# Seven block products in place of eight for m W_o in a hybrid decoder layer, with the norm chains rewritten and moved

## The chip, the core and the metric

One core of a Trainium2 chip runs the whole program: TensorE (PE) multiplies, VectorE (DVE), ScalarE (ACT) and GpSimd (POOL) work on SBUF and PSUM, SyncE (SP) issues DMAs. The metric is the device time of one execution in microseconds (us), median of several. Numbers are fp32 on the outside; lower is better.

## What is computed

One decoder layer for 512 tokens of width 1024. Cut to what matters:

```python
h = rms_norm(x, g_pre_mix)
q, k, v, cb, cc, cu, ga, gc = split(h @ w_in)
y_attn = stick_breaking_attention(q, k, v) @ w_attn_out      # 8 heads x 64
y_conv = (cb * causal_depthwise_conv(cc * cu)) @ w_conv_out  # 512 channels
m = sigmoid(ga + b) * y_attn + sigmoid(gc + b) * y_conv
x = x + rms_norm(m @ w_o, g_post_mix)                        # w_o: 1024 x 1024
x = x + rms_norm(relu(rms_norm(x, g_pre_mlp) @ w_up) ** 2 @ w_down, g_post_mlp)   # 4096 wide
x = x + sigmoid(rms_norm(x, g_ple) @ w_ple_gate) * (p @ w_ple_proj)
```

## The kernel before

Each fp32 operand is split into a high part, rounded to PE's format by ACT, and the rest, made by DVE (`split`, lines 63 to 66); `mm3` (lines 90 to 93) multiplies high x high, high x low and low x high into one PSUM bank, so every product is three matmuls. A weight block comes by a DMA on SP's queue into one of four `raw` buffers and is split into two of 15 `w` buffers of 128 x 1024 (`weights`, `wcols`, `wrow`; `w4` is such a buffer as 2 x 512). Sixteen `big` buffers of 128 x 2048 hold what lives longer; PSUM has eight banks of 128 x 512, taken by `bank()`.

The stages on PE, in order: the head (norm of x, v), attention in four steps j of two heads each, mix in eight steps j of 128 columns of m (two gate products, y_conv's and y_attn's), W_o, p's product with w_pp, W_up, W_down, the last gate. PE's and SP's instructions run in the order in which the program writes them (`manual_schedule`, line 41). DVE, ACT and POOL are ordered by a scheduler when the program is built, from its own costs and the order of the text; `tc.issue_after(ins)` puts the instructions of a block behind `ins` on its engine. On every engine that order is then fixed, and an instruction that waits holds those behind it.

W_down is already multiplied as 2 x 2 blocks by seven products instead of eight, and W_up (from column block 2) as well: sums and differences of blocks are multiplied and added up onto each other's banks. W_down's sums of weight blocks are made early: `make_sums` (line 296) loads two blocks of w_down (512 KB each), makes four differences of 128 x 512 on DVE or POOL, and its results are saved to DRAM by the next `save_sums` (line 289). It is called 16 times: twice before attention, once in each step of attention, once in each of mix (on POOL from j = 2 on), and twice in W_o.

Around the change. In mix (line 468) each m block [128 channels x 512 tokens] is split into `m_h` and `m_l`. At j = 3 x is loaded again (`xr`, four DMAs of 512 KB), at j = 6 p and w_pp, at j = 7 p is turned by eight PE transposes (line 497). `rows` (line 501) is W_o: for the first four blocks of k all four token tiles and both column halves, into eight banks; then, token tile by token tile, the last four blocks of k, and behind each tile its `chain1`: `residual` (line 539) squares both banks on ACT, adds the sums up, takes the power -1/2 on POOL, scales and multiplies by the gain on DVE, adds x, squares again, scales again. `turn2` (line 563) turns a token tile's 1024 normed values by eight transposes into two banks and splits them; turn2(0) and turn2(1) stand in W_o, turn2(2) in p's product, turn2(3) in W_up's first matmuls. W_up's column blocks 0 and 16 go in two halves of 256 tokens, so that their upper half can start early; block 1 and 17 go whole; `relu2` (line 600) takes relu on ACT and the square on DVE. `residual1` (line 531) is the same chain behind W_down.

## Time and profile before

| | us |
|---|---|
| median of 3 runs | 737.27 (736.19 to 740.18) |
| the profiled execution | 735.77 |
| its span, first to last instruction | 734.0 |
| PE busy | 725.5 |
| DVE busy | 518.3 |
| ACT busy | 379.3 |
| POOL busy | 93.8 |

The profile is of one execution. Its span leaves out what lies before the first and behind the last instruction. "Busy" is the time in which at least one instruction of an engine was under way; matmuls overlap, so a matmul's busy time is longer than the distance to the next. In a row of a group, after the bar, stand the total busy time, the mean of one in ns, and the idle time of the engine just before them with what ended it. `L91` is line 91 of the kernel; `ps<-whi,mh` says that `ps` is written from `whi` and `mh`.

### The profile page before, as it was taken

The page shows a single profiled execution, that of the slowest core. Times are in us where ns is not written, and L with a number is a line of the kernel's source. Part 1 is how long each engine was busy: PE and PEld are TensorE (multiplying, and loading weights), DVE is VectorE, ACT ScalarE, POOL GpSimd, SP SyncE. Part 2 cuts the span into 40 slices and gives each one's busy share as a digit, 9 for nine tenths or more (in the row PEclk, how much of TensorE's full clock was granted, in tenths as well). Part 3 has the DMA queues.
Part 4 walks back from the last instruction along what each step waited for, and adds up shares of the span by engine and source line. Part 5 has one row for each costly group of instructions (what it writes and reads, how often), then busy time and mean ns, then how long its engine had stood idle before and what let it go on. Part 6 is the DMA issues. An engine that isn't in the chain of part 4 may idle for free.

```text
span 734.0 us, 10311 instructions
## 1 busy us (share of the span) xinstructions
PE 725.5 (99%) x3976; PEld 628.9 (86%) x3976; DVE 518.3 (71%) x644; ACT 379.3 (52%) x595; POOL 93.8 (13%) x120
## 2 busy tenths in 40 slices
PE   8999999999999999999999999999999999999997
PEld 7888788888888888888899999999988888888886
DVE  6777886968555534734789988976799778269762
ACT  6245446352434323433856777756867476256431
POOL 1106061433225220001100000000000000001100
PEclk9999999999999999999999999999999999999999
DMA  8595627154999966752424445523455767577311
GB/s 315 171 303 166 184 96 225 35 200 144 290 346 328 282 217 243 250 165 72 153 92 115 116 117 142 138 66 111 147 172 185 238 223 231 179 242 268 127 57 58
DMA packets 112105, 132.29 MB, mean 180 GB/s; under 512 B 4116, under 2 KB 82744, under 8 KB 111032
## 3 DMA queue, kind: packets, MB, share of 16 engines
q1 hardware_dynamic: 111464, 127.43, 54.8%
q10 hardware_dynamic: 592, 4.20, 1.4%
q8 instruction: 31, 0.51, 0.3%
q14 instruction: 18, 0.15, 0.1%
HBM read 108.55 MB, written 23.07 MB: 179 GB/s over the span
## 4 chain that ended last, share of the span: by engine, by line
PE 96%; DVE 1%; DMA 1%; ACT 1%; issue 0%; POOL 0%; DVEq 0%; SPq 0%; ACTq 0%; POOLq 0%
PE ps L91 30%; PE ps L92 30%; PE ps L93 30%; DMA raw<-in_w_conv_out_dram 1%; PE ps L340 1%; PE ps L388 1%; PE ps L374 1%; PE ps L182 1%; DVE wlo L65 1%; PE ps L568 1%; PE ps L141 0%; PE ps L201 0%; PE ps L223 0%; ACT whi L64 0%; PE ps L497 0%
## 5 line engine op out<-in xcount | busy, mean ns | idle before, releaser
L65 DVE TENSOR_TENSOR wlo<-raw,whi 128x512 fp32r<-128x512 f32 (+1 forms) x84 | 79.2, 964 | 54.0 <-ACT whi L64 42.0
L91 PE MATMUL ps<-h1h,whi 128*128 128x512 f32 x288 | 113.3, 393 | 0.9 <-DVE st L65 0.9
L93 PE MATMUL ps<-h1h,wlo 128*128 128x512 f32 x288 | 112.2, 390 | 0.0
L92 PE MATMUL ps<-h1l,whi 128*128 128x512 f32 x288 | 112.2, 389 | 0.0
L64 ACT CAST whi<-raw 128x512 fp32r<-128x512 f32 (+1 forms) x84 | 65.4, 808 | 60.8 <-DMA raw<-in_w_in_dram 29.0
L91 PE MATMUL ps<-w,sb 128*128 128x512 f32 x216 | 84.1, 389 | 0.0
L93 PE MATMUL ps<-w,sb 128*128 128x512 f32 x216 | 84.0, 389 | 0.0
L92 PE MATMUL ps<-w,sb 128*128 128x512 f32 x216 | 84.0, 389 | 0.0
L65 DVE TENSOR_TENSOR w<-raw,w 128x1024 fp32r<-128x1024 f32 x56 | 67.7, 1221 | 21.2 <-PE ps L92 10.2
L64 ACT CAST w<-raw 128x1024 fp32r<-128x1024 f32 x56 | 58.5, 1052 | 36.1 <-PE ps L93 13.6
L133 POOL TENSOR_TENSOR rs<-ms,mhalf 128x1 f32<-128x1 f32 x20 | 14.6, 729 | 440.0 <-DVE ms L129 364.7
L91 PEld LDWEIGHTS ps<-h1h,whi 128*128 128x128 f32 x288 | 54.1, 188 | 12.5 <-DVE st L65 1.1
L93 PEld LDWEIGHTS ps<-h1h,wlo 128*128 128x128 f32 x288 | 54.1, 188 | 11.4
L92 PEld LDWEIGHTS ps<-h1l,whi 128*128 128x128 f32 x288 | 54.1, 188 | 10.9
L92 PE MATMUL ps<-h2l,us 128*128 128x256 f32 x224 | 63.4, 283 | 0.0
L91 PE MATMUL ps<-h2h,us 128*128 128x256 f32 x224 | 63.4, 283 | 0.0
L93 PE MATMUL ps<-h2h,us 128*128 128x256 f32 x224 | 63.4, 283 | 0.0
L65 DVE TENSOR_TENSOR us<-raw,us 128x1024 fp32r<-128x1024 f32 x42 | 50.7, 1220 | 7.9 <-ACT us L64 7.8
L64 ACT CAST us<-raw 128x1024 fp32r<-128x1024 f32 x42 | 43.4, 1050 | 17.1 <-PE ps L93 6.3
L93 PEld LDWEIGHTS ps<-w,sb 128*128 128x128 f32 x216 | 40.5, 188 | 8.5
L92 PEld LDWEIGHTS ps<-w,sb 128*128 128x128 f32 x216 | 40.5, 188 | 8.4
L91 PE MATMUL ps<-tb,us 128*128 128x256 f32 x168 | 47.7, 284 | 0.0
(206 smaller groups left out, 1650.8 us busy)
## 6 DMA issues: line engine op xcount, KB each, us to landing
raw<-in_w_in_dram SPq DMA_DIRECT2D x36, 512.0 KB, 7.0
w<-in_w_down_dram SPq DMA_DIRECT2D x32, 512.0 KB, 4.5
wsum<-w SPq DMA_DIRECT2D x32, 512.0 KB, 4.0
raw<-in_w_up_dram SPq DMA_DIRECT2D x32, 512.0 KB, 4.2
raw<-wsum SPq DMA_DIRECT2D x32, 512.0 KB, 5.3
raw<-in_w_down_dram SPq DMA_DIRECT2D x24, 512.0 KB, 4.1
raw<-in_w_o_dram SPq DMA_DIRECT2D x8, 512.0 KB, 5.9
raw<-in_w_ple_gate_dram SPq DMA_DIRECT2D x8, 512.0 KB, 7.1
```

The costliest lines, as they stand in the source:

```text
L64: a = nc.scalar.copy(hi, src)
L65: b = nc.vector.tensor_tensor(lo, src, hi.bitcast(F32), op=ALU.subtract)
L91: nc.tensor.matmul(ps, lh, rh, start=start, stop=False, skip_group_check=onto)
L92: nc.tensor.matmul(ps, lh, rl, start=False, stop=False, skip_group_check=onto)
L93: nc.tensor.matmul(ps, ll, rh, start=False, stop=stop, skip_group_check=onto)
L133: nc.gpsimd.tensor_tensor(r, m, mhalf, op=ALU.pow)
L182: nc.tensor.transpose(warm[:, 0:P], ident, ident)
L340: nc.tensor.matmul(ps[h][:, c0:c0 + n], st[r, a, qb * P:(qb + 1) * P], st[r, b, 0:n], start=i == 0, stop=i == 2)
L374: nc.tensor.transpose(ps[:, c0 + (qb - kb) * P:c0 + (qb - kb + 1) * P], w[:, o:o + P], ident)
L388: nc.tensor.matmul(ps[:, kb * P:S], lhs, wt[i][:, c0:c0 + n], start=(kb == 0 and i == 0), stop=(kb == NT - 1 and i == 1))
L568: nc.tensor.transpose(ps[:, i * P:(i + 1) * P], hn1[t][g][:, i * P:(i + 1) * P], ident)
```

## The change

W_o's and m's 2 x 2 blocks (512 x 512 of W_o; 256 tokens x 512 channels of m) are multiplied by seven products in the order 1, 2, 6, 7, 5, 3, 4. Each takes two token tiles and four blocks of k. Three take blocks of W_o as they are, loaded as 256 x 512 pieces; the others take differences, made in mix by `wo_sums` from three pieces each at j = 2 and 4 (`ot[5]`, `ot[6]`, `ot[7]`), and `ot[4]` when product 2's pieces are split. m stays in fp32 (`mf`); blocks for products 1, 2 and 4 are split in mix, the others in W_o from sums that mix makes at j = 5 and 7. Products 6, 5 and 3 are added onto product 1's bank, 4 onto 7's, and product 2 onto a bank into which ACT copies product 1.

The two `make_sums` of W_o move to attention, steps j = 1 and 2. xr, p and w_pp are loaded in W_o, and p is turned there, behind product 7's first half. The chains multiply by the gain beside the square and add x in the scaling step, for both norms. The upper tokens' chains (t = 0, 1) run behind product 3, their turns in p's product; the lower ones' (t = 2, 3) are queued behind turn2(0)'s and turn2(1)'s splits, and their turns stand in W_up. Column block 1 joins 0 and 16 in going by halves; relu's square goes to ACT; sums of the normed tokens are made in another order, and the first two `up_load` are queued behind splits.

```diff
@@ attention, mix @@
         make_sums(nc.vector)
+        if j in (1, 2):
+            make_sums(nc.vector)
...
+    def wo_sums(i):
+        b = [w4() for _ in range(3)]
+        for t, (r, c) in zip(b, ((0, 0), (0, 1), (1, 1))):
+            wo_block(t, r, c, i)
+        t1, t2, t3 = (ot[n][:, 2 * i:2 * i + 2] for n in (5, 6, 7))
+        for r_, x_, y_ in ((t1, b[1], b[0]), (t3, b[2], b[1]), (t2, b[2], t1)):
+            nc.vector.tensor_tensor(r_, x_, y_, op=ALU.subtract)
...
-        nc.vector.tensor_tensor(sa, sa, sc, op=ALU.add)
-        split(m_h[j // 4][:, j % 4], m_l[j // 4][:, j % 4], sa)
-        if j == 3:
-            for t in range(NT):
-                nc.sync.dma_start(xr[t // 2][:, t % 2, :], x[t * P:(t + 1) * P, :])
...
+        nc.vector.tensor_tensor(mj, sa, sc, op=ALU.add)
+        for n in ((1,), (2, 4))[j // 4]:
+            split(mq[n][:, 0, v], mq[n][:, 1, v], mquart(n)[:, v])
+        if j in (2, 4):
+            wo_sums(j // 2 - 1)
+        if j in (5, 7):
...
+            nc.vector.tensor_tensor(m21, m21, m22, op=ALU.add)
+            nc.vector.tensor_tensor(m11, m21, m11, op=ALU.subtract)
+            nc.vector.tensor_tensor(m12, m12, m11, op=ALU.subtract)
+            nc.vector.tensor_tensor(m22, m22, m11, op=ALU.subtract)
@@ chains @@
+    def residual(xt, c, parts, gpost, gnext, ss=()):
+        for hf, a_ in parts:
+            ss = [*ss, square(a_)]
+        flat = c.rearrange("p a b -> p (a b)")
+        for hf, a_ in parts:
+            nc.vector.tensor_tensor(flat[:, hf], a_, gpost[:, hf], op=ALU.mult)
+        r = rstd_from(ss)
+        nc.vector.scalar_tensor_tensor(xt, flat, r, xt, op0=ALU.mult, op1=ALU.add)
+        s2 = square(xt)
+        nc.vector.scalar_tensor_tensor(flat, xt, rstd_from([s2]), gnext, op0=ALU.mult, op1=ALU.mult)
+        return [c[:, 0], c[:, 1]]
@@ W_o @@
-    rows(NK, lambda k: (m_h[k // 4][:, k % 4], m_l[k // 4][:, k % 4]), w_o, 4, chain1)
+    def wo_done(n, t):
+        ps = oacc[n, t]
+        if n == 1:
+            oacc[2, t] = bank()
+            oc[t], oc[t + 2] = w4(), w4()
+            nc.scalar.copy(oacc[2, t], ps)
+        elif n == 2:
+            oss[t] = square(ps)
+            nc.vector.tensor_tensor(oc[t][:, 0], ps, gpm[:, HALF[0]], op=ALU.mult)
+        elif n == 6:
+            nc.scalar.copy(oc[t + 2][:, 0], ps)
+        elif n == 5:
+            nc.scalar.copy(oc[t + 2][:, 1], ps)
+            nc.vector.tensor_tensor(oc[t + 2][:, 1], oacc[7, t], oc[t + 2][:, 1], op=ALU.add)
+        elif n == 3:
+            chain1(t)
+        elif n == 4:
+            nc.vector.tensor_tensor(oc[t + 2][:, 0], ps, oc[t + 2][:, 0], op=ALU.add)
+    plan_o = [(n, i) for n in ORDER for i in range(2)]
+    THEN = {(1, 0): save_sums, (2, 0): load_xr, (2, 1): load_pp, (7, 0): turn_p}
+    no = 0
+    for n, i in plan_o:
+        while no < min(len(plan_o), plan_o.index((n, i)) + 4):
+            wo_left(plan_o[no][0])
+            wo_load(*plan_o[no])
+            no += 1
+        for t in range(2):
...
+            for k in (2 * i, 2 * i + 1):
+                mm3(oacc[n, t], mq[n][:, 0, k, ts], mq[n][:, 1, k, ts], *ob[n, k],
+                    k == 0 and n in (1, 7), k == 3, n not in (1, 7))
+            if i == 1:
+                wo_done(n, t)
+        if (n, i) in THEN:
+            THEN[n, i]()
@@ p's product, W_up @@
-            if (t, h_) == (1, 0):
-                turn2(2)
+            if (t, h_) in ((0, 0), (1, 1)):
+                turn2(t)
+                with tc.issue_after(hold[0].ins), tc.issue_after(hold[1].ins):
+                    chain1(t + 2)
...
-        nc.vector.scalar_tensor_tensor(af[c // 4][:, c % 4], ps, 0.0, r, op0=ALU.max, op1=ALU.mult)
+        nc.scalar.activation(af[c // 4][:, c % 4], r, AF.Square)
...
-        for c in (0, NJ):
+        for c in (0, NJ, 1):
...
-            if half == 0 and c == 0:
-                turn2(3)
+            if half == 0 and c != 1:
+                turn2(2 if c == 0 else 3)
...
-    up_load(FIRST)
+    relu2(1 + NJ, proj(wcols(w_up, (1 + NJ) * P), hm))
+    with tc.issue_after(hold[0].ins), tc.issue_after(hold[1].ins):
+        hold[:] = up_load(FIRST)
     save_sums()
```

## Rows read from the trace of the kernel before

**Rows 1.** The page: busy time of the engines; the chain that ended last, by engine.
```profile
PE 725.5 (99%) x3976; PEld 628.9 (86%) x3976; DVE 518.3 (71%) x644; ACT 379.3 (52%) x595; POOL 93.8 (13%) x120
...
PE 96%; DVE 1%; DMA 1%; ACT 1%; issue 0%; POOL 0%; DVEq 0%; SPq 0%; ACTq 0%; POOLq 0%
```

**Rows 2.** Waits of PE over the whole span: us in total, times, longest.
```profile
PE ps L91 <- DVE st L65: 0.9, 1, 0.9
...
PE ps L92 <- DVE oyl L65: 0.7, 1, 0.7
```

**Rows 3.** Groups of instructions (count, busy us, mean ns); timeline of PE in W_o.
```profile
L91 PE MATMUL ps<-whi,mh 128*128 128x512 f32 x64 | 25.1, 392 | 0.0
...
307.96 0.39 PE L91 MATMUL ps<-whi,mh 128*128 128x512 f32 x1
...
308.64 0.39 PE L91 MATMUL ps<-whi,mh 128*128 128x512 f32 x1
```

**Rows 4.** Timeline of PE, first matmuls of W_up: start us, length us, instruction.
```profile
365.32 0.28 PE L91 MATMUL ps<-h2h,whi 128*128 128x256 f32 x1
...
365.68 0.28 PE L91 MATMUL ps<-h2h,whi 128*128 128x256 f32 x1
```

**Rows 5.** Timeline of PE around the turns of the normed tokens, same columns.
```profile
345.37 1.04 PE L568 MATMUL ps<-ident,tmp 128*128 128x128 f32 x8
...
356.48 0.39 PE L93 MATMUL ps<-wph,pt 128*128 128x512 f32 x1
357.01 1.29 PE L568 MATMUL ps<-ident,tmp 128*128 128x128 f32 x8
```

**Rows 6.** Busy time by stretch: W_o, p's product, W_up; us and counts, clock, DMA share, GB/s.
```profile
306.60:352.50 45.90, 45.90 (x216) 38.25 (x214) 23.27 (x40) 18.16 (x38) 2.75 (x5) 1.00 0.44 140
352.50:365.00 12.50, 12.32 (x60) 9.88 (x59) 11.09 (x21) 11.73 (x25) 2.78 (x3) 1.00 0.38 136
...
390.00:530.00 140.00, 140.00 (x1165) 139.77 (x1165) 115.14 (x158) 99.78 (x169) 0.00 (x0) 1.00 0.43 124
```

**Rows 7.** Groups of instructions: DVE's, ACT's and POOL's kinds that the change uses.
```profile
L65 DVE TENSOR_TENSOR w<-raw,w 128x1024 fp32r<-128x1024 f32 x56 | 67.7, 1221 | 21.2 <-PE ps L92 10.2 <-ACT w L64 8.5 <-issue 2.0
...
L64 ACT CAST w<-raw 128x1024 fp32r<-128x1024 f32 x56 | 58.5, 1052 | 36.1 <-PE ps L93 13.6 <-DMA raw<-wsum 12.4 <-DMA raw<-in_w_down_dram 7.3
...
L309 DVE TENSOR_TENSOR w<-w,w 128x512 f32<-128x512 f32 x30 | 19.9, 691 | 8.8 <-PE ps L92 6.5 <-DMA w<-in_w_down_dram 2.2
...
L133 POOL TENSOR_TENSOR rs<-ms,mhalf 128x1 f32<-128x1 f32 x20 | 14.6, 729 | 440.0 <-DVE ms L129 364.7 <-DVE ms L131 75.3
...
L686 ACT COPY tmp<-ps 128x256 f32<-128x256 f32 x14 | 5.2, 372 | 0.7 <-PE ps L93 0.7
...
L533 DVE SCALAR_TENSOR_TENSOR w<-w,rs,gb 128x1024 f32<-128x1024 f32 x4 | 5.1, 1282 | 1.9 <-POOL rs L133 1.9
...
L591 ACT COPY pp<-ps 128x512 f32<-128x512 f32 x8 | 4.4, 620 | 0.4 <-PE ps L93 0.4
...
L125 ACT ACTIVATE junk<-xr 128x1024 bf16<-128x1024 f32 x4 | 4.2, 1061 | 8.3 <-DVE xr L545 8.3
...
L129 DVE TENSOR_SCALAR ms<-ss 128x1 f32<-128x1 f32 x16 | 2.4, 149 | 7.0 <-ACT junk L125 6.9
```

**Rows 8.** Busy time by stretch: attention j = 1, and the start of mix.
```profile
88.00:122.50 34.50, 34.50 (x184) 29.12 (x182) 27.21 (x31) 16.63 (x32) 11.27 (x16) 1.00 0.44 132
...
189.00:230.00 41.00, 40.27 (x182) 33.26 (x181) 21.87 (x26) 15.13 (x21) 15.25 (x12) 1.00 1.07 338
```

**Rows 9.** Timeline of DVE and PE: splits of W_up, a gate weight's split and its use.
```profile
379.92 3.49 DVE L65 TENSOR_TENSOR tb<-hf,tb 128x1024 fp32r<-128x1024 f32 x3
...
207.42 1.94 DVE L65 TENSOR_TENSOR wlo<-raw,whi 128x1024 fp32r<-128x1024 f32 x1 [3.51 <-ACT whi L64]
...
224.79 0.39 PE L91 MATMUL ps<-h1h,whi 128*128 128x512 f32 x1
```

**Rows 10.** Waits of SP's queue: us in total, times, longest.
```profile
SPq L303 <- PE ps L93: 76.5, 11, 16.7
```

More of the change, by code (lines that the diff above doesn't have):

```diff
@@ L555, in hybrid_block @@
+    WHOLE, HALF = slice(0, D), (slice(0, 512), slice(512, D))
     gpm = gain(g_post_mix)
     gml = gain(g_pre_mlp)
+    xr = [bigt([P, 2, D], F32, "xr") for _ in range(2)]
+    pt = bigt([P, 4, S], name="pt")
+    wpb = [bigt([P, 2, D], name="wpb") for _ in range(2)]
     hn1 = {}
@@ L561, in hybrid_block @@
     pps = [sums.tile([P, 2, D], F32, name=f"pps{i}") for i in range(2)]
+    hold = []
     def turn2(t):
@@ L569, in turn2 @@
             p3 = ps.rearrange("p (a b) -> p a b", b=P)
-            split(h2[0][g][:, :, tok], h2[1][g][:, :, tok], p3)
+            hold[:] = split(h2[0][g][:, :, tok], h2[1][g][:, :, tok], p3)
             nc.scalar.copy(hf[t // 2][:, g, :, (t % 2) * P:(t % 2 + 1) * P], p3)
-    def chain1(t, accs):
-        hn1[t] = residual(xr[t // 2][:, t % 2, :], accs, gpm, gml)
+    ORDER = (1, 2, 6, 7, 5, 3, 4)
+    RIGHT = {1: (0, 0), 2: (1, 0), 3: (1, 1)}
+    ONTO = {6: 1, 5: 6, 3: 5, 4: 7}
+    ob, osum = {}, {}
@@ new lines, in wo_load @@
+    def wo_load(n, i):
+        two = slice(2 * i, 2 * i + 2)
+        if n in RIGHT:
+            src = raws.tile([P, 2, 512], F32, tag="raw", name="raw")
+            wo_block(src, *RIGHT[n], i)
+        else:
+            src = ot[n][:, two]
+        lo, hi = w4(F32R), w4(F32R)
+        split(hi, lo, src)
+        if n == 2:
+            if i == 0:
+                ot[4] = bigt([P, 4, 512], F32, name="ot")
+            nc.vector.tensor_tensor(ot[4][:, two], src, ot[6][:, two], op=ALU.subtract)
+        for u in range(2):
+            ob[n, 2 * i + u] = hi[:, u], lo[:, u]
@@ new lines, in wo_left, with load_xr, load_pp @@
+    def wo_left(n):
+        if n not in mq:
+            mq[n] = bigt([P, 2, 4, 256], name="mq")
+            split(mq[n][:, 0], mq[n][:, 1], mquart(n))
+    def load_xr():
+        for t in range(NT):
+            nc.sync.dma_start(xr[t // 2][:, t % 2, :], x[t * P:(t + 1) * P, :])
+    pf = {}
+    def load_pp():
+        pf[0] = raws.tile([P, NT, 256], F32, tag="raw", name="raw")
+        nc.sync.dma_start(pf[0], p[0].rearrange("(t p) d -> p t d", p=P))
+        for kk in range(2):
+            raw = raws.tile([P, D], F32, tag="raw", name="raw")
+            nc.sync.dma_start(raw, w_pp[kk * P:(kk + 1) * P, :])
+            split(wpb[kk][:, 0], wpb[kk][:, 1], raw)
@@ new lines, in turn_p, with chain1 @@
+    def turn_p():
+        for kk in range(2):
+            ps = bank()
+            for t in range(NT):
+                nc.tensor.transpose(ps[:, t * P:(t + 1) * P], pf[0][:, t, kk * P:(kk + 1) * P], ident)
+            split(pt[:, kk], pt[:, 2 + kk], ps)
+    oacc, oc, oss = {}, {}, {}
+    def chain1(t):
+        xt = xr[t // 2][:, t % 2, :]
+        if t < 2:
+            hn1[t] = residual(xt, oc[t], [(HALF[1], oacc[3, t])], gpm, gml, [oss[t]])
+        else:
+            hn1[t] = residual(xt, oc[t], [(WHOLE, oc[t].rearrange("p a b -> p (a b)"))], gpm, gml)
@@ L705, in up_mm @@
                 nc.vector.tensor_tensor(quarter(1, 0, g), quarter(1, 0, g), quarter(1, 1, g), op=ALU.add)
-    up_load(FIRST)
+    relu2(1 + NJ, proj(wcols(w_up, (1 + NJ) * P), hm))
+    with tc.issue_after(hold[0].ins), tc.issue_after(hold[1].ins):
+        hold[:] = up_load(FIRST)
     save_sums()
-    for c in range(1, FIRST):
-        for h in range(2):
-            relu2(c + h * NJ, proj(wcols(w_up, (c + h * NJ) * P), hm))
+    right(7, f12)
     split(*rt[5], f11)
+    nc.vector.tensor_tensor(f21, f21, f22, op=ALU.subtract)
+    right(4, f21)
     order = sorted((7 * c + 2 * i, c, n) for c in range(FIRST, NJ) for i, n in enumerate((1, 2, 6, 7, 5, 4, 3)))
     for _, c, n in order:
-        if n == 6 and c + 1 < NJ:
+        if n == 6 and c == FIRST:
+            with tc.issue_after(hold[0].ins), tc.issue_after(hold[1].ins):
+                up_load(c + 1)
+        elif n == 6 and c + 1 < NJ:
             up_load(c + 1)
```

112 lines of the change are left out of this document (28 added, 84 removed).

## The prediction

> **What bounds the kernel now.** I read the page's busy table and its chain first. TensorE (PE) is busy for 725.5 of 734.0 us and the chain that ended last is 96% PE [rows 1]; the reader is to see that nothing but fewer or shorter PE instructions, or less PE idle time, can shorten this program. Then the waits, PE alone: five in all, and the two that lie behind the start, 0.9 and 0.7 us, are late VectorE (DVE) splits [rows 2]. There is next to no idle time left to win, and each new wait shows in full.
>
> So I price PE by its pitch, not by its busy time, which counts overlapping ends twice. Three 512-column matmuls start within 0.68 us, 0.227 us each [rows 3]; three 256-column ones within 0.36 us, 0.120 us each [rows 4], a little more than half. W_o now is 64 matmuls on each of three lines [rows 3], 192 in all.
>
> **The change, part by part.**
>
> *Seven products.* Each has 2 token tiles x 4 blocks of k x 3 = 24 matmuls of 512 columns; seven make 168. 24 fall away: 24 x 0.227 = **-5.44 us**, all on the path.
>
> *W_up's entry.* Column block 1 goes in two halves too: 24 x 0.227 = 5.44 becomes 48 x 0.120 = 5.76: **+0.32 us**. The four relu steps of that stretch leave DVE for ScalarE (ACT): about 4 x 0.69 us less DVE work [rows 7], hidden both ways.
>
> *The lower tokens' turn.* At 356 us PE now stands still before turn2(2): 0.53 from the last matmul to the first transpose, against a pitch of 0.227 (0.30), and the eight transposes take 1.29 instead of 1.04 (0.25) [rows 5]. Chain and turn move to W_up's entry, further behind each other: **-0.55 us**. What is late next: hn1[0], turned after the first block of the p product. From the first upper bank's end to that turn PE has 6 + 24 + 6 matmuls = 8.2 us; the chain is a half-wide square (taken as the 512-wide copy's 0.62), two additions of 0.15, two powers of 0.73, two wide DVE steps of 1.28 and a wide square of 1.06, 6.0 us [rows 7]. For chain1(3), queued behind turn2(1)'s splits by issue_after, PE has four p blocks, two runs of 24 half-wide matmuls and a turn, 5.4 + 5.8 + 1.0 = 12.2 us; splits (0.62 and 0.69) and chain (the same with a wide multiplication of 1.22 in the square's place, 6.6) take 7.9. I take 0 for both. ACT carries the copies of p's banks meanwhile (eight of 0.62, as now).
>
> *One DVE step less in each chain.* x is added in the scaling step, and the gain is multiplied beside the square: 1.22 us less per chain [rows 7]. In the last stages no wait of PE stands among [rows 2], so chain2's gain is worth 0.
>
> *Hand-over of banks.* Product 2 adds onto a bank that ACT has just copied from product 1's, product 3 onto the bank that ACT is copying out of after product 5: four hand-overs (two token tiles each). No row shows a copy from PSUM to PSUM; its bounds are 0.37 (256 wide) and 1.05 (1024 wide), and I take 0.62, the 512-wide copy out of PSUM [rows 7]. PE turns from tile 0 to tile 1 first: six matmuls, 1.36 us. A matmul's 0.39 [rows 3] ends 0.16 after the next one starts; 0.16 + 0.62 = 0.78 fits, if ACT is free. With a 1.05 cast just begun it doesn't: 0.78 + 1.05 - 1.36 = 0.47 each, 1.9 for four. ACT is busy for 18.2 of 45.9 us there [rows 6], and W_up's hand-overs (copies of 0.37 under 12 matmuls of 0.12) left PE 140.00 of 140 us busy [rows 6, 7]. I take **+0.3**; ends 0 and 1.9.
> A page of the Trainium skill, Perfetto Trace Analysis (Optimizing Tensor Performance, Matmuls), speaks against this part: independent groups of matmuls should rotate through different banks, so that the evacuation of one overlaps the matmuls of the next. Here the next group goes to the bank being evacuated; by that rule the upper end would be paid. This trace bears it out only so far that W_up's copies, which have another product between, cost nothing.
>
> *DVE and ACT in W_o.* Behind the last m block DVE has 18 operations 1024 wide (ten splits of W_o's blocks and sums, four of m's, two differences for ot[4], two of w_pp), 18 x 1.22 = 22.0; 14 of 512 (the last product's two steps, the sums of j = 7, two of pt, six evacuations), 14 x 0.69 = 9.7; and the two upper chains, 2 x 3.6 = 7.1 [rows 7]: 38.8 us, while PE has 168 x 0.227 + 0.9 (p's turn, which moves in here) = 39.0. Before it was 23.3 in 45.9 [rows 6]. That is the change's tightest spot. Part of it (the first sums' splits, ot[4]) can go ahead of W_o, since the blocks land in mix; I take 0, and the bound below as a rival.
>
> *Mix and attention.* wo_sums adds six differences of 1.22 and six transfers of 512 KB; the sums of m add 8 x 0.69, and each split of 512 columns becomes one or two of 256. PE never reads any of it in mix. DVE was busy for 21.9 of 41 us in the stretch with the fullest DMA queues [rows 8]: covered. Two make_sums go from W_o to attention, j = 1 and 2: 2 x (4 x 0.69) on DVE, two loads and two saves each on SP's queue. DVE was busy for 27.2 of 34.5 us there and PE for all of it [rows 8]; with 2.8 it is 30.0: covered, without it 2.8 each. On SP these saves wait for DVE's sums with the next weights behind them. xr (2 MB) and p's loads (1.5 MB) leave mix for W_o, where the DMA engines have 140 GB/s to move [rows 6].
>
> **Sum.** -5.44 + 0.32 - 0.55 + 0.3 = -5.4 us. The profiled execution took 735.77 (its span is 734.0), 1.5 below the median of the runs, 737.27. Against the median: **731.9 us** (against the profiled one 730.4).
>
> **The rivals.**
> 1. *DVE becomes the bound in W_o* (19%). For: 38.8 against 39.0. In the chains' stretch before DVE worked 11.1 of 12.5 us [rows 6], 11% idle on small waits; on 39 us that is 4.4, so it would end 38.8 + 4.4 - 39.0 = 4.2 late. Against: neighbours overlap (three of 1.22 in 3.49, start to start 1.13 [rows 9]), which takes 2.7 off: 1.5. Middle 3: **735**.
> 2. *Each bank hand-over is paid* (8%): 1.9 instead of 0.3, and 0.4 for the additions out of banks behind the same casts: **733.9**. For: ACT's order is fixed ahead of time. Against: its 40% load. This is the case that the Trainium skill's rule above describes.
> 3. *SP's queue holds up mix* (8%): the time goes to the other side. The three loads of wo_sums(0) stand in SP's order between j = 2's saves and j = 3's weights, and need three weight buffers at once where DMA moves 338 GB/s [rows 8]. SP's waits for a buffer at make_sums' loads were 11, mean 7.0, longest 16.7 us [rows 10]. One of the longest and one mean one, and 1.5 MB at 338 GB/s (4.7) make 28.4; the gate weight behind was split by 209.4 and first used at 224.8, 15.4 ahead [rows 9]. PE would stand for 13.0: 731.9 + 13.0 = **744.9**. It decides from a hold of 10.7 us at these loads; it passes the time of before at 16. Against: DMA loses xr in the next step, 2 MB, and buffers come free with each product.
> That the matmuls would not fall away is no case: 168 follows from the loops.
>
> **How the numbers follow.** The forecast has 65%: 732, and between 729.4 (nothing for hand-overs, the 0.7 of [rows 2] gone, and the runs at the level of the profiled one) and 733.5. A measurement of this kernel tells about 0.5% (3.7 us) from no change: faster is under 733.6, slower over 741.0. Faster: 65%. Same: rivals 1 and 2, 27%. Slower: rival 3, 8%. The range goes from the forecast's lower end to rival 1's upper one (731.9 + 4.2): 729.4 to 736.2; it leaves out rival 3 and some of the forecast's own tails.
>
> **What would show it.** Right: 56 matmuls on each line of mm3 in W_o; PE without gaps over 0.3 us from the end of mix to W_up; the gap at 356 gone; p's turn amid W_o. DVE over 80% busy in W_o and ACT's copies into PSUM near 0.6. Rival 1: PE waits for DVE splits of W_o's blocks or m's. Rival 2: waits for ACT's copies at the first matmul of products 2 and 3. Rival 3: waits for DVE or ACT splits between 205 and 260 us, with SP standing at wo_sums. Wrong altogether: a 512-column pitch other than 0.227, or a gap of over 2 us at any turn.

## The result, and the profile after

| | before | after |
|---|---|---|
| median, us (20 runs each) | 736.76 (735.29 to 741.17) | 740.56 (736.71 to 744.63) |
| the profiled execution | 735.77 | 739.98 |
| its span | 734.0 | 738.2 |

The ratio, after to before on the same chip, with its 95% interval, is 1.0049 [1.0035, 1.0063]: slower by 0.5%, where 0.7% faster was forecast. The page of after, busy time and chain, answers [rows 1]:

```profile
PE 722.9 (98%) x3976; PEld 626.7 (85%) x3976; DVE 541.8 (73%) x657; ACT 391.9 (53%) x608; POOL 94.6 (13%) x120
...
PE 80%; DVE 7%; DMA 5%; ACT 2%; issue 2%; POOL 2%; SPq 0%; DVEq 0%; POOLq 0%; ACTq 0%
```

PE has less to do (722.9, was 725.5) and the program takes longer: the chain is 80% PE, was 96%. So the time is in waits. PE's waits (us in total, times, longest), beside [rows 2]:

```profile
PE ps L91 <- DVE st L65: 3.9, 3, 1.8
PE ps L551 <- DVE w L528: 1.8, 2, 1.3
...
PE ps L91 <- ACT tmp L772: 1.1, 1, 1.1
PE ps L91 <- ACT tmp L765: 0.8, 1, 0.8
PE ps L91 <- DVE tmp L774: 0.8, 1, 0.8
PE ps L92 <- DVE oyl L65: 0.7, 1, 0.7
```

Where they lie is read from the start of each stage's first matmul (us, from the traces; e1, e8 and e11 are experiments below):

| first matmul of | before | after | e1 | e8 | e11 |
|---|---|---|---|---|---|
| scores, j = 2 | 122.56 | 124.17 | 122.45 | 123.66 | 121.58 |
| scores, j = 3 | 156.85 | 160.57 | 156.74 | 158.83 | 155.87 |
| mix | 191.04 | 194.77 | 190.93 | 193.02 | 190.06 |
| W_o | 307.19 | 310.14 | 306.26 | 307.35 | 304.38 |
| p's product | 352.53 | 349.11 | 345.24 | 346.33 | 343.70 |
| W_up | 364.97 | 363.35 | 359.46 | 360.57 | 356.87 |
| W_up's seven products | 388.26 | 388.54 | 384.69 | 385.79 | 384.24 |
| W_down | 529.67 | 533.75 | 530.07 | 528.62 | 526.43 |
| end of the span | 733.98 | 738.23 | 734.54 | 732.90 | 731.14 |

After loses 3.7 us in attention, wins 0.8 in mix (p's turn has left it) and 6.4 between W_o's first matmul and p's (5.4 by the products; p's turn came, turns of hn1 went), loses 1.8 in p's product and 1.9 in W_up's first blocks (turns that moved in, two waits, the 0.32), and 3.8 in W_up's seven products.

W_o went as forecast. Its groups (count, busy us, mean ns, idle before) and the stretch by engine:

```profile
L91 PE MATMUL ps<-w,mq 128*128 128x512 f32 x56 | 21.9, 391 | 0.0
...
L623 ACT COPY ps<-ps 128x512 f32<-128x512 f32 x2 | 1.2, 584 | 0.9 <-PE ps L93 0.9
```

```profile
310.00:349.00 39.00, 39.00 (x178) 32.41 (x177) 31.90 (x40) 26.58 (x42) 1.86 (x2) 1.00 0.48 154
```

56 matmuls a line without idle PE, the copy from bank to bank 0.58 us, DVE at 31.9 of 39 us. 310.14 to 349.11 is 38.97, which is 168 x 0.227 and 0.8 for p's turn.

The profile tells how attention's waits come about. SP's and DVE's timelines of after, j = 1 (start, length, instruction, idle before):

```profile
86.89 0.38 SPq L295 DMA_DIRECT2D wsum<-w  x1
87.36 1.29 SPq L306 DMA_DIRECT2D w<-in_w_down_dram  x2
88.74 18.91 SPq L71 DMA_DIRECT2D raw<-in_w_in_dram  x5
107.70 1.09 SPq L295 DMA_DIRECT2D wsum<-w  x2
```

```profile
110.70 0.69 DVE L65 TENSOR_TENSOR oyl<-tmp,oyh 128x512 fp32r<-128x512 f32 x1
113.00 2.36 DVE L65 TENSOR_TENSOR wlo<-raw,whi 128x1024 fp32r<-128x1024 f32 x2 [1.62 <-DMA wsum<-w]
115.28 0.68 DVE L65 TENSOR_TENSOR st<-ps,st 128x512 fp32r<-128x512 f32 x1
```

SP issues four weights of the step, and holds the fifth until a raw buffer comes free, at 107.3. The saves of the extra sums stand behind it (107.7). The split at 113.00 needs a weight buffer that such a sum holds, and waits for its save to land; st's split stands behind that one and another in DVE's order, and PE waits for st. DVE itself had time: it was idle 1.6 us just there. The held load has a second way to st: it landed at 111.6, and ACT casts that weight just ahead of st. ACT's and PE's timelines there:

```profile
111.68 1.05 ACT L64 CAST whi<-raw 128x1024 fp32r<-128x1024 f32 x1 [1.37 <-DMA raw<-in_w_in_dram]
112.63 0.57 ACT L64 CAST st<-ps 128x512 fp32r<-128x512 f32 x1
...
116.02 0.50 PE L91 MATMUL ps<-h1h,whi 128*128 128x512 f32 x1 [1.44 <-DVE st L65]
```

### The profile page after: what moved, and what is told of

The parts are those of the page before. It is cut to its first block, busy times and chain, and to the rows that moved or that the text cites. A ratio compares the mean times of both kernels' runs of the same rounds, so it can differ in the third digit from the quotient of the medians.

```text
span 738.2 us, 10350 instructions
## 1 busy us (share of the span) xinstructions
PE 722.9 (98%) x3976; PEld 626.7 (85%) x3976; DVE 541.8 (73%) x657; ACT 391.9 (53%) x608; POOL 94.6 (13%) x120
## 4 chain that ended last, share of the span: by engine, by line
PE 80%; DVE 7%; DMA 5%; ACT 2%; issue 2%; POOL 2%; SPq 0%; DVEq 0%; POOLq 0%; ACTq 0%
PE ps L91 26%; PE ps L92 25%; PE ps L93 25%; DMA raw<-in_w_up_dram 2%; DMA wsum<-w 1%; DMA raw<-in_w_conv_out_dram 1%; DVE wlo L65 1%; DVE us L65 1%; DMA w<-in_w_down_dram 1%; POOL rs L136 1%; DVE keep L357 1%; DVE xr L526 1%; DVE w L528 1%; PE ps L185 1%; PE ps L391 1%
## 5 line engine op out<-in xcount | busy, mean ns | idle before, releaser
L65 DVE TENSOR_TENSOR wlo<-raw,whi 128x1024 fp32r<-128x1024 f32 (+1 forms) x68 | 69.0, 1033 | 45.3 <-ACT whi L64 33.1
L64 ACT CAST whi<-raw 128x1024 fp32r<-128x1024 f32 (+1 forms) x68 | 56.2, 850 | 77.2 <-DMA raw<-in_w_in_dram 50.1
L65 DVE TENSOR_TENSOR w<-raw,w 128x1024 fp32r<-128x1024 f32 x62 | 74.8, 1220 | 25.7 <-PE ps L92 13.7
L64 ACT CAST w<-raw 128x1024 fp32r<-128x1024 f32 x62 | 64.6, 1052 | 41.6 <-PE ps L93 15.3
L136 POOL TENSOR_TENSOR rs<-ms,mhalf 128x1 f32<-128x1 f32 x20 | 16.6, 829 | 435.2 <-DVE ms L132 361.9
```

What stands on the lines that cost most here:

```text
L64: a = nc.scalar.copy(hi, src)
L65: b = nc.vector.tensor_tensor(lo, src, hi.bitcast(F32), op=ALU.subtract)
L136: nc.gpsimd.tensor_tensor(r, m, mhalf, op=ALU.pow)
```

## Experiments on attention

All medians and ratios (to the kernel before, on the same chip, 95%) in one table; "e2 before + sums", "e13 before + raw buffer" and the like name the kernel that was edited. The span is that of one profiled execution:

| kernel | median | ratio | span |
|---|---|---|---|
| e1 sums in W_up | 737.67 | 1.0011 [0.9987, 1.0034] | 734.5 |
| e2 before + sums | 741.36 | 1.0048 [1.0022, 1.0073] | 737.6 |
| e3 relu on DVE | 741.78 | 1.0057 [1.0033, 1.0081] | 739.4 |
| e4 later turns | 744.29 | 1.0087 [1.0053, 1.0121] | 741.6 |
| e5 tb first | 744.48 | 1.0099 [1.0080, 1.0118] | 743.5 |
| e6 upper chains abreast | 736.56 | 0.9996 [0.9982, 1.0011] | 734.5 |
| e7 e5 and e6 | 743.96 | 1.0094 [1.0071, 1.0117] | 743.2 |
| e8 sums in place | 735.75 | 0.9988 [0.9976, 1.0000] | 732.9 |
| e9 e8, saves earlier | 736.49 | 0.9993 [0.9976, 1.0010] | 735.8 |
| e10 e9, turns | 736.97 | 1.0000 [0.9983, 1.0016] | 733.7 |
| e11 e9, a fifth raw buffer | 734.22 | 0.9955 [0.9940, 0.9970] | 731.1 |
| e12 after + raw buffer | 736.77 | 0.9992 [0.9973, 1.0012] | 738.8 |
| e13 before + raw buffer | 736.91 | 0.9996 [0.9979, 1.0014] | 734.8 |
| e14 e11, later turn2(3) | 737.61 | 1.0005 [0.9987, 1.0023] | 734.6 |
| e15 e11, lower chains abreast | 741.03 | 1.0053 [1.0032, 1.0075] | 739.1 |
| e16 e11, tb ahead | 734.25 | 0.9955 [0.9939, 0.9970] | 731.2 |
| e17 e16, later turn2(3) | 734.60 | 0.9961 [0.9946, 0.9977] | 731.4 |
| e18 e16, shorter chains | 731.56 | 0.9931 [0.9909, 0.9954] | 729.7 |

Every edit also lets the scheduler order DVE's and ACT's work anew, and single waits shift with it: from the scores of j = 1 to those of j = 3 after takes 72.4 us, e2, e3 and e4, whose sums, loads and buffers there are the same, 71.5 to 72.4. Differences below about 1 us between two profiles are no evidence of a cause.

In the expectations a wait is the distance between two starts on PE less the usual pitch, which comes out 0.1 to 0.3 us longer than the profile's idle time.

**e1 and e2: the sums out of attention, and into it alone.**

```diff
@@ e1 @@
-        if j in (1, 2):
-            make_sums(nc.vector)
...
         up_mm(c, n)
+        if n == 3 and c in (5, 8):
+            make_sums(nc.gpsimd)
+        elif n == 3 and c == 11:
+            save_sums()
@@ e2, on the kernel before @@
-            if k in (1, 3):
-                make_sums(nc.vector)
-            if k == 4:
+            if k == 0:
                 save_sums()
...
+        if j in (1, 2):
+            make_sums(nc.vector)
```

> The changed kernel, but the two extra make_sums leave attention and are made by GpSimd in W_up, behind column blocks 5 and 8. Theory: in attention they cost 3.7 us (the scores of j = 2 and 3 start 1.7 and 3.7 us later than before), so these starts come back to 122.6 and 156.9 us, PE's wait there for st (1.65 and 2.06 us in the changed kernel) falls under 0.5, and the span goes from 738.2 to 734.5 (to within 0.5 us of the kernel before). In W_up GpSimd is idle, and the sums should cost nothing there. Rival (attention is late for another cause of the change, as more weights' loads or another order of DVE's work from the mix's new parts): scores 2 and 3 stay at 124.2 and 160.6, and the span at 738.

> The kernel before, with this one move of the change: the two make_sums of W_o (k = 1 and 3) are made in attention behind j = 1 and 2. Theory: the move alone costs attention what the changed kernel shows, +3.7 us at the scores of j = 3 (156.9 becomes 160.6), nothing comes back later since W_o has no idle PE to fill: span 734.0 becomes 737.7, ratio to before 1.005. Rival (the extra sums are covered as predicted, and the loss hangs on the change's other parts): scores 3 at 156.9, span 734.0, ratio 1.000.

Both spans came within 0.1 us of the theory (734.5 and 737.6), and e1's scores are back at 122.45 and 156.74. Two make_sums in attention cost 3.7 us with the rest of the change and without it. That e1's span met 734.5 so closely is partly luck: its seven products of W_up take 145.4 us, as long as after's (145.2), but for another reason. After's waits behind 400 us are gone, and waits of 2.2 us at 430, 436 and 467 us stand in their place, beside GpSimd's sums, which "should cost nothing there"; what these do stands in the last section.

**e8, e9, e11, e12, e13: what they wait for.** e8 lets each set of sums overwrite the blocks that it read; e9 saves them ahead of the fifth weight; e11 moves one 4 KB buffer from the weights' pool to the raw loads'.

```diff
@@ e8 @@
-        o = [w4(), w4()]
-        t1, t2, t3, t4 = (o[i // 2][:, i % 2] for i in range(4))
...
+        for r, x_, y_ in ((0, 1, 0), (1, 3, 1), (3, 3, 0), (2, 2, 3)):
+            eng.tensor_tensor(q[r], q[x_], q[y_], op=ALU.subtract)
@@ e9, on e8 @@
         tb = wtrans(wb)
+        save_sums()
@@ e11, on e9; e12, on after; e13, on before @@
-    wts = ctx.enter_context(tc.tile_pool(name="wts", bufs=15))
-    raws = ctx.enter_context(tc.tile_pool(name="raws", bufs=4))
+    wts = ctx.enter_context(tc.tile_pool(name="wts", bufs=14))
+    raws = ctx.enter_context(tc.tile_pool(name="raws", bufs=5))
```

> The changed kernel with the extra make_sums left in attention, but every make_sums writes its four differences over the blocks it loaded: two weight buffers a set instead of four; DVE's work, the loads and the saves are the same. Theory A (buffers: DVE's split of a weight waits there for a buffer that a sum holds until its save has landed, and st's split stands behind it): scores of j = 2 and 3 come back to within 0.7 us of 122.6 and 156.9, the span to about 735. Theory B (DVE's added work of 2.8 us per step, or SP's order of loads and saves): they stay 1.6 and 3.7 us late, span 738.

> e8, with save_sums() called in attention ahead of conv_c's weight as well, so that SP issues the saves of the sums, made by 95 us, before the fifth weight of the step (which has to wait for a raw buffer until 104.5) and not behind it. DVE's work and the bytes are those of e8. Theory (what is left of attention's loss in e8, 0.9 and 0.8 us in front of j = 2 and 3, is still the buffer that a cast of a weight gets only when a save has landed, 111.25 us): the saves land by about 101, the losses fall under 0.3 each, scores of j = 3 at 157.0, the span from 732.9 to about 731.2. Rival (the rest is the 2.8 us that DVE has more to do in each of these steps): the waits stay, span 732.5 to 733.

> e9 with one buffer of 4 KB a partition moved from the weights' pool (15 to 14) to that of raw loads (4 to 5). Theory of W_up's entry: the waits of 1.0 us at 388 and of 0.5 to 1.3 later come from DVE being late with its sums, so that a raw buffer comes free late and then the load's landing stands on the path (DVE idle 2.0 us in e8, 3.4 in the changed kernel, until a load issued at 401 has landed). With a fifth raw buffer the next load starts earlier, that idle time of DVE goes, and so do the waits behind 400 us (0.5); the 1.0 at 388, which no load holds, stays. Rival (the loads are not on the path): the waits behind 400 stay. In attention one weight buffer less may bring back up to 1 us by the same rule as e8.

> The changed kernel with nothing but e11's one buffer moved (weights' pool 15 to 14, raw loads 4 to 5); the extra make_sums stay in attention, each with four weight buffers, saved where the change saves them. Theory R (the choke is the raw pool: the fifth weight's load of a step stands on SP until a raw buffer is free, and the saves, the sums' buffers and the next splits stand behind it): attention's loss of 3.7 us goes to under 0.5 and W_up's waits behind 400 us (1.3, 0.9) to under 0.3; the turns' waits stay; span 738.2 to 731 to 732.5. Theory W (the weights' buffers that the sums hold): with one less of these the waits for st stay at 1.6 and 2.1 or grow, span 737 to 740.

> The kernel before with that same moved buffer, nothing of the change. PE waits there for little that a raw buffer could mend (1.1 at 79 us, 0.9 at 201): span 734.0 to between 732.0 and 733.5, ratio 0.997 to 0.999. So e11's 731.1 beside it tells what the change itself is worth once its loads are no longer held up: if this kernel came out at e11's level, the seven products would have brought nothing.

e8 took away half of the loss (scores of j = 3 at 158.83). e9's theory fell: with the saves issued earlier PE waited for st as long as in e8 (2.1 us). Ahead of st's split DVE now waits for no save and no load, only for GpSimd's beta (0.43) and ACT's cast of oyh (0.69). So e9 by itself speaks for its rival, DVE's added work; e11, which has the same work and loses nothing, speaks against it. With e11 the loss is gone; its SP timeline of the same step:

```profile
86.83 6.30 SPq L71 DMA_DIRECT2D raw<-in_w_in_dram  x4
93.24 3.95 SPq L295 DMA_DIRECT2D wsum<-w  x2
97.24 0.46 SPq L71 DMA_DIRECT2D raw<-in_w_in_dram  x1
```

The fifth weight leaves at 97.24, 10 us earlier than in after, and the sums are saved in passing. e12 tells the two pools apart. PE's waits for st in attention, after, e8 and e12:

```profile
PE ps L91 <- DVE st L65: 3.9, 3, 1.8
```

```profile
PE ps L91 <- DVE st L65: 2.1, 3, 0.8
```

```profile
PE ps L91 <- DVE st L65: 0.6, 1, 0.6
```

From the scores of j = 1 to those of j = 3 after takes 72.4 us, before 68.6, e8 70.4, e12 69.8, e11 68.6. Neither pool alone does it: the fifth raw buffer is worth 2.6, the sums in place 2.0, both together all 3.8 (e11 has e9's earlier saves too; e9 alone takes 71.2). Neither theory of e12 came out whole. Against W, the waits for st fell to 0.6. Of R, the waits behind 400 us went, but attention still lost 1.2 us and not under 0.5, the turns' waits grew from 1.8 to 2.7, and the span of 738.8 lies in W's range. That span is high by some 3.4 us for another reason, two stretches at a lower clock (last section); the median is 3.8 us under after's. So the raw buffer is the larger part, and the weights' buffers have a share.

e13 shows that the buffer by itself is nothing to the kernel before (0.9996). That is a net: its attention begins 1.0 us earlier, and 1.7 us of new waits for h2's splits stand at W_up's entry. e11 beside it, 0.9955, is 0.4%, some 3 us: so much the change as a whole brings when loads and sums are not in its way, with e8's and e9's edits, which the kernel before was not given. What the seven products alone bring was not measured. e11 is faster than both kernels.

## Experiments on the turns and W_up's entry

Behind W_o two waits are left in e11 (its waits of PE, 340 to 400 us):

```profile
PE ps L551 <- DVE w L528: 2.7, 2, 2.5
PE ps L91 <- ACT tmp L765: 0.8, 1, 0.8
```

The same two are in after, at the turns and at W_up's entry; with waits behind 400 us that e11 does not have. DVE's timeline of after at the second of the upper tokens' chains, and at W_up's third column block:

```profile
348.79 1.28 DVE L528 SCALAR_TENSOR_TENSOR w<-xr,rs,gb 128x1024 f32<-128x1024 f32 x1 [0.45 <-POOL rs L136]
349.99 0.68 DVE L524 TENSOR_TENSOR w<-ps,gb 128x512 f32<-128x512 f32 x1
...
355.59 1.28 DVE L528 SCALAR_TENSOR_TENSOR w<-xr,rs,gb 128x1024 f32<-128x1024 f32 x1 [0.44 <-POOL rs L136]
```

```profile
408.40 0.69 DVE L742 TENSOR_TENSOR s<-raw 128x512 f32<-128x512 f32 x1 [3.44 <-DMA raw<-in_w_up_dram]
```

chain1(1) begins (L524) when chain1(0) has ended (L528): one behind the other. And in W_up DVE stands 3.4 us until a load has landed that could not leave before DVE had freed a raw buffer (left at 401.3, landed at 408.4); in e11 that idle time is gone, and with it the waits of 1.1 and 0.8 us (L772 and L774 in the list above). How much it costs varies: the load took 7.1 us, where the median of these loads is 4.2, so a slow transfer is part of the 3.4. Behind 400 us after waits 1.9; e8, e9 and e3, with four raw buffers too, wait 0.3, 0.7 and 0.8, and e11, e12 and e16, with five, not at all.

**e3 to e7, with four raw buffers.**

```diff
@@ e3, on after @@
-        nc.scalar.activation(af[c // 4][:, c % 4], r, AF.Square)
+        nc.vector.scalar_tensor_tensor(af[c // 4][:, c % 4], ps, 0.0, r, op0=ALU.max, op1=ALU.mult)
@@ e4, on after @@
-            if (t, h_) in ((0, 0), (1, 1)):
-                turn2(t)
+            if (t, h_) in ((0, 0), (2, 0)):
+                turn2(t // 2)
...
-        for c in (0, NJ, 1):
+        for c in (0, NJ, 1, 1 + NJ):
...
-            if half == 0 and c != 1:
-                turn2(2 if c == 0 else 3)
+            if half == 0 and c in (0, 1):
+                turn2(2 + c)
@@ e5, on e1 @@
     right(6, f22)
+    right(7, f12)
+    nc.vector.tensor_tensor(f21, f21, f22, op=ALU.subtract)
+    right(4, f21)
@@ e6, on e1: both upper chains, step by step @@
         elif n == 3:
-            chain1(t)
+            oss[t] = [oss[t], square(ps)]
+            nc.vector.tensor_tensor(oc[t][:, 1], ps, gpm[:, HALF[1]], op=ALU.mult)
+            if t == 1:
+                upper_chains()
```

e7 is e5 and e6.

> The changed kernel, with the relu squares of W_up's first four column blocks back on DVE, out of PSUM, as before. Theory A (W_up's entry is late because ACT has two operations per relu, so that its casts of tb and us come late): PE's waits at 391, 410 and 444 us (0.99, 1.30 and 0.94) fall under 0.4 each, the span goes to 735 to 736. Theory B (the entry is late because the lower chains and turns come later, and DVE's sums of hf with them): the waits stay within 1 us of their sum of 3.2, the span stays at 738.

> The changed kernel, with turn2(1) one block of the p product later (six matmuls of 512, 1.36 us), and turn2(3) behind the first half of column block 1 instead of NJ; as cover of its splits the fourth block goes in halves too (24 matmuls less at 0.227, 48 more at 0.120: +0.32). Theory: turn2(1) waits 1.46 and turn2(3) 0.69 us for DVE's last step of hn1; with 1.36 and 2.9 us more cover both waits fall under 0.3 us, and the span from 738.2 to 736.5. Rival (what is late moves with it: chain1(3) stands behind turn2(1)'s splits, and W_up's entry behind turn2(3)'s): the waits at the turns go, but those at 391 to 444 us grow by as much, and the span stays at 738 to 739.

> e1, with the three casts and splits of tb (and f21's sum) ahead of up_load(FIRST) again, as in the kernel before; to be set beside e1 (span 734.5). Theory: PE's waits at W_up's entry (1.0 at 387 us for ACT's copy of tmp, then 0.8, 1.1 and 0.8 at 429 to 466) come from the two tb casts that ACT makes at the moment when the first seven-product block ends, in front of that copy, and from DVE's two tb splits beside them; with the casts back in ACT's idle stretch before, the waits fall from 3.7 together to under 1 and the span to about 731.5. Rival (DVE has no time to spare between turn2(3) and that block, whatever the order): the order only changes which wait ends last, the sum stays over 3, the span at 734 to 735.

> e1, with the two upper chains emitted step by step beside each other instead of one behind the other. Theory: turn2(1) waits 1.46 us since chain1(1)'s first DVE step stands in DVE's order behind chain1(0)'s last, which itself waits for GpSimd's power; side by side, hn1[1] is ready some 3 us earlier, hn1[0] about 1 later. The wait at 351 us goes (and that before turn2(3), 0.72, shrinks, since chain1(3) is held behind turn2(1)'s splits): span 734.5 to about 732.5. Rival (DVE is simply full there): the wait moves to turn2(0) or turn2(2), the span stays at 734 to 735.

> e5 and e6 together. By both theories the three places are mended and the seven products' gain is left: 734.0 - 5.4 + 0.6 for what stays: a span of about 729.5 to 730.5, ratio to before 0.994 to 0.995. By the rivals 733 to 735.

The theories failed each time; in e3, e4 and e6 the rivals' waits came, their spans only in part. e3: the wait for ACT's copy at the entry grew from 0.8 to 1.9 us, others shrank; of its span of 739.4, 1.4 us are a wait at the last gate (703 us), which the edit does not touch. e4: both turns' waits went, 1.9 us for h2's splits and 2.0 for us came; its span is 3.4 us longer than after's and past the rival's 739, of which some 1.7 us are a stretch of lower clock behind the 1.9 (granted clock 0.75, 0.50 and 0.89 in the 2 us stretches from 364 to 370). e6, whose span is e1's: PE's waits from 330 to 400 us against e1's, no less in sum (1.0 + 0.8 + 0.8 for 1.9 + 0.8):

```profile
PE ps L549 <- DVE w L526: 1.0, 1, 1.0
PE ps L91 <- ACT tmp L777: 0.8, 1, 0.8
PE ps L549 <- DVE ms L132: 0.8, 1, 0.8
```

e5 and e7 say little: 743.5 and 743.2 lie outside both theory and rival. PE is idle for 6.2 us in each from 438 to 511 us, e1 for 2.2. GpSimd's sums end at 467, so why the waits go on to 511 stays open. The expectation had put e1's waits at 429 to 466 down to tb's casts; in e1 they stand beside GpSimd's sums. e16 repeats the edit without them.

**e10 and e14 to e18, on e9 and e11.** e10 has e6's edit too, e14 the turn of e4; e15 writes the lower chains beside each other; e16 emits hf's sums and tb's splits ahead of the second halves' relus; e17 is e16 with e14's edit and the first four weights emitted ahead; e18 is e16 with shorter chains:

```diff
@@ e10, on e9 and e6's edit @@
-            if (t, h_) in ((0, 0), (1, 1)):
+            if (t, h_) in ((0, 1), (1, 1)):
@@ e14, on e11 @@
-        for c in (0, NJ, 1):
+        for c in (0, NJ, 1, 1 + NJ):
...
-            if half == 0 and c != 1:
-                turn2(2 if c == 0 else 3)
+            if half == 0 and c in (0, 1):
+                turn2(2 + c)
@@ e15, on e14 @@
-                with tc.issue_after(hold[0].ins), tc.issue_after(hold[1].ins):
-                    chain1(t + 2)
+                if t == 0:
+                    with tc.issue_after(hold[0].ins), tc.issue_after(hold[1].ins):
+                        lower_chains()
...
-            if half == 0 and c in (0, 1):
-                turn2(2 + c)
+            if half == 0 and c in (NJ, 1):
+                turn2(2 if c == NJ else 3)
@@ e17, on e16 and e14's edit @@
+    for c in (0, NJ, 1, 1 + NJ):
+        wu[c] = wcols(w_up, c * P)
@@ e16, on e11 @@
     for half in range(2):
+        if half == 1:
+            f11 = mlp_right()
@@ e18, on e16, for t = 2 and 3 @@
-        s2 = square(xt)
-        nc.vector.scalar_tensor_tensor(flat, xt, rstd_from([s2]), gnext, op0=ALU.mult, op1=ALU.mult)
+        r2 = r if short else rstd_from([square(xt)])
+        nc.vector.scalar_tensor_tensor(flat, xt, r2, gnext, op0=ALU.mult, op1=ALU.mult)
```

> e9 with e6's upper chains beside each other, and turn2(0) one block of the p product later (e6's wait moved there, 0.9 us). Theory (order alone): no wait at turn2(0) and turn2(1), that of turn2(3) at most 1.2; against e9, 1.0 us less. Rival (DVE and GpSimd have no slack between W_o's end and turn2(3), so that a wait taken away at one turn comes back at the next one): the turns' waits stay at 2 us in sum, nothing gained over e9.

> e11, with turn2(3) behind the first half of column block 1 and the fourth block in halves as cover (+0.32 us), turn2(1) where it is. In e11 the one long wait left is turn2(3)'s, 2.67 us, for hn1[3], whose chain runs on DVE behind hn1[2]'s. Theory (that wait is the lower chains' length, and PE can fill it with work that it has anyway): it goes, less 0.32, span 731.1 to 728.8. Rival (W_up's entry is set by when DVE is through with hn1[3], whatever PE does before): the 2.3 us come back as waits between 365 and 400 us (1.0 in e11 to over 3), span at 730.5 to 731.5.

> e11, with the two lower chains beside each other behind turn2(0)'s splits (not one behind the other, the second held behind turn2(1)'s), and turn2(2) and turn2(3) behind the halves of blocks NJ and 1, the fourth in halves (+0.32). Theory: hn1[3] is ready some 3 us earlier than in e11 (366.2), hn1[2] some 1.5 later; no wait of over 0.5 at a turn, DVE is through with the lower tokens earlier too, so W_up's entry keeps its 1.0; span 728.5 to 729. Rival (DVE and GpSimd are full there): hn1[3] comes no earlier than 365, and the entry's waits grow to 3; span 730.5 to 731.5.

> e11, with hf's four sums and the three casts and splits of tb emitted ahead of the relus of the second halves, not behind them. In e11 DVE stands still 2.1 us (376.2 to 378.3) until ACT has cast the first tb; that cast's data is there from 374.4, but in ACT's order it stands behind relu(NJ), which waits for PE until 376.1; the other two casts stand in front of the copy that PE waits for at 387 (1.00 us). Theory (ACT's fixed order at W_up's entry, not a lack of DVE's time): DVE's idle 2.1 us and PE's wait of 1.0 go, that at turn2(3) (2.67) stays; span 731.1 to 730.1, ratio to before 0.994. Rival (as e5 had it, any order only moves the wait): 1 us or more comes back between 380 and 400, span 731 or more.

> e16 with e14's later turn2(3) (behind the first half of block 1, the fourth block in halves, +0.32 us), and W_up's first four weights emitted ahead of the turns, since in e14 the fourth one's cast came too late (1.94 us of wait in place of 2.67). Theory (order): the wait at turn2(3) goes with nothing in its place but up to 1 us at W_up's entry; span 730.1 to between 727.8 and 729. Rival (PE has to wait for hn1[3] and what follows from it, wherever the turn stands): the waits between 360 and 400 us stay at 2.5 us in sum, span at 730 to 731.

> e16, with a part of the computation left out: the second square, sum and power of the two lower tokens' chains (hn1[2] and hn1[3] are scaled by the first norm's factor). From the end of one DVE step to the next that is 2.0 us a chain, 4.1 for hn1[3], whose chain stands behind hn1[2]'s; little of it is DVE's time. Theory C (the length of the two chains in a row is what PE waits for): the wait at turn2(3) (2.68) goes, and W_up's entry comes with its 0.8 or less: span 731.2 to 728.0 to 728.6, as much as the seven products and little else would leave. Theory E (W_up's entry is short of ACT's and DVE's time from there on): the wait at the turn goes, but the waits between 375 and 400 us grow from 0.8 to 3; span 730.5 to 731.2.

e10: one wait of 1.9 us at a turn in place of two (1.9 together), nothing gained. e14 and e15: the wait of 2.5 us went from the turn to W_up's entry with interest. e16 freed DVE of its 2.1 us of idle time at the first cast of tb, of which 1.0 came back at a later one, and PE gained nothing. In e17 no wait at a turn is over 0.4, and the entry has it all; PE's waits from 340 to 400 us in e16, e17 and e18:

```profile
PE ps L551 <- DVE w L528: 2.7, 2, 2.5
PE ps L91 <- ACT tmp L774: 0.6, 1, 0.6
```

```profile
PE ps L93 <- DVE us L65: 1.5, 2, 0.8
PE ps L91 <- ACT us L64: 1.4, 1, 1.4
PE ps L551 <- DVE w L528: 0.2, 1, 0.2
```

```profile
PE ps L93 <- DVE us L65: 0.9, 1, 0.9
PE ps L91 <- ACT us L64: 0.3, 1, 0.3
PE ps L551 <- DVE w L528: 0.2, 1, 0.2
```

3.3, 3.1 and 1.4 us. e18 leaves out the second norm's factor of the lower tokens. That shortens each lower chain by its second square and power, on ACT and GpSimd, with hardly less work for DVE. hn1[3] is ready at 363.3 instead of 366.2, and the span fell by 1.5 us: the turn's wait went, and half of it did not come back. The ratio fell by 0.24%, which the two intervals do not separate. Its 729.7 lies between what theories C and E had said. So the waits point at the length of the two lower chains, one behind the other, and behind it at the entry's casts and splits; of the kernels here only the shorter path helped, none of the orders tried (e6, e10, e14 to e17) did. e18 also takes two squares off ACT, so the chain's length and ACT's load are not told apart. Which of ACT and DVE limits the entry itself stays open: in e17 DVE stands still for 3.1 us there, waiting for a cast that stands in ACT's order behind relus.

## Why the prediction was wrong

The seven products brought what the sum says. What failed are three steps that it put at nothing: the make_sums moved into attention (3.7 us), the turns (1.8) and, behind them, W_up's seven products (3.8). None of the three rivals came as it was written. Part by part:

- *Seven products* (-5.44): right. W_o takes its 168 matmuls and a turn. *Hand-over of banks*: the mechanism was right, and 0 would have been the better value than +0.3. The upper bound of the hand-over, which the Trainium skill's rule would pay (Perfetto Trace Analysis, Optimizing Tensor Performance, Matmuls), did not come: the copies took 0.58 us and PE waited for none.
- *The gap at 356* (-0.55) went at turn2(2), as forecast (its first transpose, at 366.23, waits for nothing); one of 1.3 us came at turn2(1), at 356.93.
- *One DVE step less in each chain* (0 for chain2): right. From W_down's first matmul to the end of the span it is 204.3 us before and 204.5 after.
- *DVE and ACT in W_o* (38.8 of 39.0): oversized; 31.9, which is 82% of the 39 us. Of the list, three operations of 1.22 went ahead into mix (3.7), and the second upper chain and product 4's two additions ran behind W_o (4.9); six splits of 512 columns of W_up's weights (4.1), which the list does not have, ran in it. Rival 1 fell with it: no wait for a split of W_o's blocks or of m's.
- *Mix and attention*: the step that failed first; it put the two moved make_sums at 0, and they cost 3.7 us (e1, e2). "DVE was busy for 27.2 of 34.5 us there and PE for all of it [rows 8]; with 2.8 it is 30.0: covered." DVE was busy for 28.8 of 34.5 us there in after, less than that, and PE came 3.7 us late: the load was covered, the order was not. The text did say that on SP "these saves wait for DVE's sums with the next weights behind them", and priced it at nothing; in after it was the other way round, the saves waited behind a weight that had no raw buffer (sent at 107.3; with a fifth raw buffer at 97.2, and no loss). That buffers are the cause is shown by e8, e11 and e12; how much each link of the chain carries, next to the scheduler's new order, is not. Rival 3 had this mechanism, but put it at wo_sums in mix, where e1 (mix from 190.93 to 306.26, 115.3 us; before 116.2 with p's turn) shows no price.
- *The lower tokens' turn*: put at 0, it cost 1.8 us of waits in after. For hn1[0] 6.0 us were forecast; the chain took 7.6 (from ACT's square at 342.5 to DVE's end at 350.1), with other DVE work between its steps, and the cover of 8.2 took it: turn2(0) did not wait. For turn2(1) no sum was made; chain1(1) begins when chain1(0) has ended, and PE waited 1.3 us. For chain1(3) 7.9 us were set against a cover of 12.2. Cover and chain were right (12.4 and 6.6 in e11), but chain1(3) stands behind chain1(2): e11, where nothing before it is late, measures 13.0 for the two (353.2 to 366.2), hn1[3] came 14.9 us behind turn2(1), and PE waited 2.5. e18's waits say that this length is on the path.
- *W_up's entry* (+0.32 and "hidden both ways"): right for the halves. What was left out is W_up's seven products, which take 145.2 us in after and 141.4 before: the entry, from the turns on, comes later for DVE and ACT, about 1 us of wait at the first seven-product block, and a raw buffer freed later is a load that lands later, 1.9 us more behind 400 us in this execution of after, none with a fifth buffer (e11). In e11 0.8 us are left of the 3.8.
- The sum with the measured terms: -5.44 + 0.32 - 0.55 + 3.7 (attention) + 1.8 (turns) + 3.8 (W_up's seven products) = +3.6; the span shows +4.25. Of the 0.6 between them 0.35 are the turns' two waits, which by starts are 2.15, and 0.2 lie behind W_down's first matmul.

## What to carry to other kernels

Work moved to an engine "with time to spare" is not covered by that time: ask which buffers it takes, which queue issues its loads and saves, and what stands behind them in fixed order. Where PE is 99% busy, price a moved step by the wait that each of its pools can bring: here one 4 KB buffer in the other pool took the change from 0.5% slower to no difference (1.0049 to 0.9992, e12), and, where the sums also take fewer buffers, from no difference to 0.45% faster (0.9993 to 0.9955, e9 to e11). And where two chains follow each other on the same engines, set their sum against the cover, not each by itself.
